# Trainium2 mixer layer: sums of weight quarters written in 64 small parts tied to the weight stream, and another order of the last seven products

## The chip, the cores and the metric

The kernel runs on one core of a Trainium2 chip. The metric is the device time of one execution in microseconds (us), as the median of several runs. A difference of 0.3% (about 4 us) is about what a measurement of this kernel can tell from no change.

## The reference, cut to what matters

One layer with a token length S of 512 and a width D of 2048. What matters here is the end of it:

```
mod = silu(c) @ w_ada + b_ada;  shift, scale, gate = split(mod, 3)
h = rmsnorm(x, norm_pre) * (1 + scale) + shift
proj = h @ w_in                      # q, f, v, z_a, v_b, z_b, g_a, g_b
...                                  # recurrent mixer -> y_a, pooling mixer -> y_b
merged = sigmoid(g_a) * (y_a @ w_proj_a) + sigmoid(g_b) * (y_b @ w_proj_b)
out = merged @ w_out                 # 512x2048 times 2048x2048
x = x + gate * rmsnorm(out, norm_post)
```

## The kernel before, in words

Each float32 product is made as three products of rounded halves: a block of weights of 512 KB is loaded by SyncE (SP) into a tile `raw`, ScalarE (ACT) rounds it into `hi` (L177), VectorE (DVE) subtracts to get `lo` (L178), and TensorE (PE) multiplies hi by hi, hi by lo and lo by hi (L91). `w_piece` does this; each of `raw`, `hi` and `lo` has four buffers, and the blocks of all stages go through them in one line. Every engine and every DMA queue works through its own list in order.

The stage of the gates (tiles `g_ps`, stored as `sig`) is the columns g_a and g_b of `h @ w_in`: sixteen steps, (b, m) with b of 0 and 1 and m of 0, 2, to 14, each of four blocks (96 matmuls). The first of them and four steps for z_a (`za`) come earlier; fifteen follow without another stage between them. Into these steps two more streams are laid. The rows of the adaLN gate: 64 loads of 256 KB into tiles `gw`, six behind the four weight blocks of a step on SP's queue (`gate_rows`), each of which DVE multiplies into the tile `gate` (L621, L623); in DVE's list they stand between the `lo` of the weight blocks. After each sixteen rows `gate_finish` sends two small matmuls (`gate_ps`), eight in all. And the sums of quarters of w_out, which the last stage needs: for each half pr of the output columns four DRAM tiles `wsum` of 1024x512, named f12, f3, f4, f2, made by a plain DMA from DRAM to DRAM and then one that adds onto it, both on GpSimd's (POOL) queue (L882). f3 adds f12, and f4 adds f3. Two such DMAs are issued in each of eight steps, 2 MB each, 16 in all; nothing ties them to the progress of PE.

Then y_a and y_b (tiles `y`, 16 loads of 256 KB on POOL's queue, L892) are split, and the stage `pa`/`pb` multiplies them by w_proj_a and w_proj_b, with the same weight stream of 512 KB blocks and no `gw`.

The last stage is `merged @ w_out` by Strassen-Winograd: for each half of the columns seven products, numbered 1 to 7, of four weight blocks and 48 matmuls each, in the order of the table `ORDER`. Products 1, 2, 3 and 6 read parts of `merged` or w_out as they are; 4, 5, 6 and 7 need token operands `op4`, `op3`, `op1`, `op2`, which `op_34`, `op_2`, `op_1` compute on DVE and ACT during the first half. A finished product is added into the output tiles `og` (rows of tokens t, 0 to 3, and column blocks j) as `INTO` says. As soon as an `og` tile is complete its squares are summed on ACT (L1069) and it is multiplied by the gate on DVE (L1070). As soon as the four tiles of a t are complete, `finish` takes the root of the mean square (ACT L248, DVE L249 to L252), multiplies and adds x again (L1031, four instructions), and stores (L1032). x comes by `x_again` on POOL's queue. The last product of all, number 4 of the second half, loads all its four blocks first and does all of its first token tile (t 0) before the second (t 1).

Of the kernel before, what the change touches and what calls it, by code (L numbers as in the profile page):

```python
# [9 lines left out]
F32 = mybir.dt.float32  # L10
# [3 lines left out]
ALU = mybir.AluOpType  # L14

P = 128
D = 2048
S = 512
KT = D // P
# [6 lines left out]
ZA_AT = 2  # L26
# [8 lines left out]
def trunk(ctx, tc, x, c, w_ada, b_ada, norm_pre, norm_post, w_in, lower_bounds, hgrn_norm,  # L35
          pool_w, pool_scale, w_proj_a, w_proj_b, w_out, out):
    nc = tc.nc
# [3 lines left out]
    const = ctx.enter_context(tc.tile_pool(name="const", bufs=1))  # L41
# [8 lines left out]
    def t_h(name, dt=F32R):  # L50
        return act.tile([P, S], dt, tag="h", bufs=32, name=name)

    def t_s(name, dt=F32):
        return act.tile([P, S], dt, tag="s", bufs=32, name=name)

    def t_w(name, n=S, dt=F32):
        return act.tile([P, 544], dt, tag="w", bufs=10, name=name)[:, :n]
# [8 lines left out]
        return pg.tile([P, S], F32, tag="pg", name=name)  # L66

    last_load, last_pool = [None], [None]

    def load(dst, src):  # L70

        if last_load[0] is None:
            d = nc.sync.dma_start(dst, src)
        else:
            with tc.issue_after(last_load[0]):
                d = nc.sync.dma_start(dst, src)  # L76
        last_load[0] = ins_of(d)
# [4 lines left out]
    def ins_of(d):  # L82
        return getattr(d, "ins", d)
# [38 lines left out]
    def finish_heads(n):  # L122
        while steps and len(heads_done) < n:
            tick(1)
# [12 lines left out]
    scan_mask = const.tile([P, S], F32, name="scan_mask")  # L137
# [33 lines left out]
    def w_piece(name, src, k0, nk, c0, n, eng=None):  # L171

        raw = ring.tile([P, nk, n], F32, tag="raw", bufs=4, name=f"{name}_raw")
        load(raw, src[k0 * P:(k0 + nk) * P, c0:c0 + n].rearrange("(k p) n -> p k n", p=P))
        hi = ring.tile([P, nk, n], F32R, tag="whi", bufs=4, name=f"{name}_hi")
        lo = ring.tile([P, nk, n], F32R, tag="wlo", bufs=4, name=f"{name}_lo")
        last_w[0] = ins_of(nc.scalar.copy(hi, raw))  # L177
        (eng or (nc.gpsimd if steps and next(turn) else nc.vector)).tensor_sub(lo, raw, hi.bitcast(F32))  # L178
        return hi, lo

    def split(name, src, alloc, eng=None):
# [81 lines left out]
    with tc.high_priority():  # L263
        for t in range(TT):
            for j in range(4):
                junk = t_w(f"junk_{t}_{j}")
# [69 lines left out]
    def in2(name, c0):  # L336
        outs = [t_ps(f"{name}_ps0"), t_ps(f"{name}_ps1")]
        proj2(name, w_in, KT, c0, hh, hl, outs)
        return outs
# [227 lines left out]
    def gate_a(h, p):  # L567
        sz = t_w(f"sza_{h}")
        nc.scalar.activation(sz, p, AF.Silu)
        sz_a[h] = sz  # L570

    def finish_a(h):
        y = o_sb[h]
        nc.vector.scalar_tensor_tensor(y, y, vec[:, R_HN + h:R_HN + h + 1], sz_a[h], op0=ALU.mult, op1=ALU.mult)
        last_pool[0] = ins_of(nc.gpsimd.dma_start(y_dram[0][h], y))
# [38 lines left out]
    def gate_rows(j, k):  # L614

        if k == 0:
            gate[j] = t_w(f"gate_{j}")
        t = t_w(f"gw_{j}_{k}")
        load(t, w_ada[k * P:(k + 1) * P, 2 * D + j * S:2 * D + (j + 1) * S])
        if k == 0:  # L620
            nc.vector.tensor_scalar(gate[j], t, c_act[:, 0:1], None, op0=ALU.mult)  # L621
        else:
            nc.vector.scalar_tensor_tensor(gate[j], t, c_act[:, k:k + 1], gate[j], op0=ALU.mult, op1=ALU.add)  # L623
# [40 lines left out]
    for k0 in range(2, KT, 2):  # L664
        first, last = (needs[k0 - 2] if k0 > 2 else 1) + 1, needs[k0]
# [25 lines left out]
    start, t = [], 0.0  # L691
# [6 lines left out]
    for it in seq:  # L698
        if it[0] == "w":
            n = it[1]  # L700
# [58 lines left out]
    for n, (name, k0, k_first, k_last) in enumerate(chunks):  # L759
        t, fresh, ends = start[n], needs[k0] == n, k0 + 1 == k_last  # L760
# [84 lines left out]
    HK = D // 2  # L845
    wsum = [[dram.tile([HK, S], F32, name=f"wsum_{i}_{pr}") for i in range(4)] for pr in range(2)]
    quarter = lambda pr, i, j: w_out[i * HK:(i + 1) * HK, (2 * pr + j) * S:(2 * pr + j + 1) * S]
    wsum_steps = []
    for pr in range(2):
        f12, f3, f4, f2 = wsum[pr]  # L850
        for dst, first, second in ((f12, quarter(pr, 0, 1), quarter(pr, 1, 1)), (f3, quarter(pr, 0, 0), f12),
                                   (f4, quarter(pr, 1, 0), f3), (f2, quarter(pr, 0, 0), quarter(pr, 0, 1))):
            wsum_steps += [(dst, first, {}), (dst, second, {"accum_op": ALU.add, "max_dma_last_dim": 8192})]

    wsum_steps = [s for pr in range(2) for acc in (0, 1) for s in wsum_steps[8 * pr + acc:8 * pr + 8:2]]

    sig = [[None] * KT, [None] * KT]
    for b, off in ((0, OFF_GA), (1, OFF_GB)):
        for m in range(0, KT, 2):
            if (b, m) == (0, ZA_AT):  # L860
                for h in range(0, NH, 2):
                    o2 = in2(f"za{h}", OFF_ZA + h * P)
                    gate_a(h, o2[0]); gate_a(h + 1, o2[1])
                    if h < 6:
                        finish_heads(h + 2)
                        finish_a(h); finish_a(h + 1)
            o2 = in2(f"g{b}_{m}", off + m * P)
            if (b, m) == (0, ZA_AT + 2):
                finish_heads(NH)
                finish_a(6); finish_a(7)  # L870

            first = ZA_AT // 2 + 2
            step = b * KT // 2 + m // 2 - first
            for i in range(max(0, step * GATE_PER), min(4 * KT, (step + 1) * GATE_PER)):
                gate_rows(i // KT, i % KT)
                if i % KT == KT - 1:
                    gate_finish(i // KT)
            if b * KT + m >= 8 and wsum_steps:
                for _ in range(2):
                    dst, src, kw = wsum_steps.pop(0)  # L880
                    with tc.issue_after(last_pool[0]):
                        last_pool[0] = ins_of(nc.gpsimd.dma_start(dst, src, **kw))  # L882
            for r in range(2):
                sig[b][m + r] = t_s(f"sig{b}_{m + r}")
                nc.scalar.activation(sig[b][m + r], o2[r], AF.Sigmoid)
# [94 lines left out]
    xr = [[None] * 4 for _ in range(TT)]  # L980
    ss = [const.tile([P, 4], F32, name=f"ss_{t}") for t in range(TT)]
    ms3 = [const.tile([P, 1], F32, name=f"ms3_{t}") for t in range(TT)]
    junk = const.tile([P, S], mybir.dt.bfloat16, name="ojunk")

    def product(pr, n, banks, last):
        form, b = PRODUCTS[n]
# [47 lines left out]
    def t_acc(pr, block, name):  # L1034
        return t_s(name) if pr == 0 else t_h(name, F32) if block == (0, 0) else t_w(name)

    def x_again(t):
        for j in range(4):
            xr[t][j] = t_h(f"xr_{t}_{j}", F32)
            nc.gpsimd.dma_start(xr[t][j], x[t * P:(t + 1) * P, j * S:(j + 1) * S])  # L1040

    ORDER = [[1, 3, 2, 4, 5, 7, 6], [1, 3, 6, 2, 7, 5, 4]]
    after = {(0, 1): op_34, (0, 3): op_2, (0, 2): op_1, (1, 6): lambda: x_again(2), (1, 2): lambda: None,
             (1, 7): lambda: (x_again(3),), (1, 5): lambda: (x_again(0), x_again(1))}
    for pr, order in enumerate(ORDER):
        left = {blk: sum(b == blk for n in order for b, _ in INTO[n]) for blk in ((0, 0), (0, 1), (1, 0), (1, 1))}
        banks, begun = {}, set()
        for n in order:
            alloc = t_pg if n in (1, 3) else t_ps
            banks[n] = banks[ONTO[n]] if n in ONTO else [alloc(f"out_{pr}_{n}_{tt}") for tt in range(2)]  # L1050
            for tt in product(pr, n, banks, (pr, n) == (1, 4)):
                p = banks[n][tt]
                for (i, jj), sign in INTO[n]:
                    t, j = 2 * i + tt, 2 * pr + jj
                    if ((i, jj), tt) not in begun:
                        begun.add(((i, jj), tt))
                        og[t][j] = t_acc(pr, (i, jj), f"og_{t}_{j}")
                        if sign > 0:
                            nc.scalar.copy(og[t][j], p)
                        else:  # L1060
                            nc.scalar.activation(og[t][j], p, AF.Copy, scale=-1.0)
                    elif sign > 0:
                        nc.vector.tensor_add(og[t][j], p, og[t][j])
                    else:
                        nc.vector.tensor_sub(og[t][j], og[t][j], p)
                    left[i, jj] -= 1 if tt else 0
                    if left[i, jj] == (0 if tt else 1):
                        at_ss = place(t, j)
                        nc.scalar.activation(junk, og[t][j], AF.Square, accum_out=ss[t][:, at_ss:at_ss + 1])  # L1069
                        nc.vector.tensor_mul(og[t][j], og[t][j], gate[j])  # L1070
                        if pr == 1 and at_ss == 2:
                            first_sums(t)
                        if at_ss == 3:
                            finish(t)
            after.get((pr, n), lambda: None)()


# [27 lines left out]
```

## Time and profile before

| | |
|---|---|
| time, median of 3 runs | 1421.37 us (1418.52 to 1421.98) |
| time of the profiled execution | 1424.94 us |
| its span, first to last instruction | 1423.2 us |
| busy: PE, DVE, ACT, POOL | 93%, 57%, 39%, 17% |
| mean granted TensorE clock | 0.974 |
| moved by DMA | 238.11 MB, mean 167 GB/s |

Busy shares are over the whole span. The stages have different limits, so a share says little of one stage. A clock of 1.00 is the higher of TensorE's two levels, 2.4 GHz, and 0.50 the lower, 1.2 GHz; a number between them is a mean over a stretch. The DMA share is the mean over 16 engines, and can pass 1.00 since the packets of one engine overlap a little.

### The profile page before, as it was taken

How to read it: one execution, taken by the hardware profiler on the slowest of the kernel's cores; microseconds unless marked ns; L12 is line 12 of the kernel's file. 1: busy time of each engine (PE TensorE's matmuls, PEld its weight loads, DVE VectorE, ACT ScalarE, POOL GpSimd, SP SyncE). 2: the span in 40 equal slices, each digit the busy share in tenths (PEclk: the TensorE clock that was granted, in tenths of full speed). 3: DMA queues.
4: the chain of work that ended last, by engine and by line, in shares of the span. 5: the costliest groups of instructions: out<-in, count | busy, mean ns of one | idle time of the engine just before them, and what ended most of it. 6: DMA issues, size and time to landing. Idle time of an engine off the chain costs nothing.

```text
span 1423.2 us, 16399 instructions
## 1 busy us (share of the span) xinstructions
PE 1328.0 (93%) x6031; PEld 1091.8 (77%) x6031; DVE 812.6 (57%) x1336; ACT 559.2 (39%) x787; POOL 246.3 (17%) x269
## 2 busy tenths in 40 slices
PE   4899999999999999999997737999999999999996
PEld 2777888888888887888876525888888888887885
DVE  4789462474957869668422223454335554587667
ACT  5544452364554564546411111222234222255552
POOL 3555401132232222223101000000001000000010
PEclk9999999999999999999998868999999999999998
DMA  9989533222223233242399999865435333336675
GB/s 310 357 271 358 183 90 104 84 74 75 86 85 111 73 97 104 75 133 89 119 327 255 286 277 248 239 192 162 156 122 166 97 96 97 104 127 199 196 255 214
DMA packets 170232, 238.11 MB, mean 167 GB/s; under 512 B 8780, under 2 KB 120484, under 8 KB 169128
## 3 DMA queue, kind: packets, MB, share of 16 engines
q1 hardware_dynamic: 155528, 188.78, 41.7%
q0 software_dynamic: 13312, 46.14, 12.0%
q10 hardware_dynamic: 1312, 2.14, 0.4%
q8 instruction: 47, 0.77, 0.2%
q14 instruction: 33, 0.27, 0.1%
HBM read 228.64 MB, written 41.94 MB: 190 GB/s over the span
## 4 chain that ended last, share of the span: by engine, by line
PE 76%; DMA 14%; DVE 7%; issue 1%; SPq 1%; ACT 1%; POOL 0%; DVEq 0%; ACTq 0%
PE g_ps L91 18%; PE out L91 8%; DMA gw<-in_w_ada_dram 8%; PE vb_ps L91 6%; PE za_ps L91 6%; PE v_ps L91 6%; PE pb L91 6%; PE pa L91 6%; PE g L91 5%; PE zb_ps L91 5%; DMA ada<-in_w_ada_dram 4%; PE q_ps L91 3%; PE lv L91 2%; DMA g_raw<-in_w_in_dram 1%; SPq L76 1%
## 5 line engine op out<-in xcount | busy, mean ns | idle before, releaser
L91 PE MATMUL g_ps<-h_hi,g_lo 128*128 128x512 f32 x512 | 205.3, 401 | 53.5 <-DVE g_lo L178 53.5
L91 PE MATMUL g_ps<-h_hi,g_hi 128*128 128x512 f32 x512 | 204.5, 399 | 0.0
L91 PE MATMUL g_ps<-h_lo,g_hi 128*128 128x512 f32 x512 | 203.2, 397 | 0.0
L177 ACT CAST g_hi<-g_raw 128x1024 fp32r<-128x1024 f32 x64 | 67.0, 1050 | 238.8 <-DMA g_raw<-in_w_in_dram 112.8
L91 PEld LDWEIGHTS g_ps<-h_hi,g_lo 128*128 128x128 f32 x512 | 98.8, 193 | 77.9 <-DVE g_lo L178 57.0
L623 DVE SCALAR_TENSOR_TENSOR gate<-gw,c_act,gate 128x512 f32<-128x512 f32 x60 | 45.1, 751 | 151.7 <-DMA gw<-in_w_ada_dram 150.7
L91 PEld LDWEIGHTS g_ps<-h_lo,g_hi 128*128 128x128 f32 x512 | 98.8, 193 | 21.2
L91 PEld LDWEIGHTS g_ps<-h_hi,g_hi 128*128 128x128 f32 x512 | 99.0, 193 | 20.6
L178 DVE TENSOR_TENSOR g_lo<-g_raw,g_hi 128x1024 fp32r<-128x1024 f32 x61 | 73.7, 1220 | 64.4 <-ACT g_hi L177 64.4
L178 DVE TENSOR_TENSOR wo_lo<-wo_raw,wo_hi 128x1024 fp32r<-128x1024 f32 x56 | 68.2, 1223 | 43.8 <-ACT wo_hi L177 43.6
L177 ACT CAST wo_hi<-wo_raw 128x1024 fp32r<-128x1024 f32 x56 | 59.0, 1054 | 68.2 <-PE out L91 51.5
L105 DVE SCALAR_TENSOR_TENSOR ada_acc<-ada,c_act,ada_acc 128x512 f32<-128x512 f32 x104 | 73.3, 750 | 7.8 <-DMA ada<-in_w_ada_dram 7.3
L1040 POOL DMA_DIRECT2D xr<-in_x_dram x16 | 8.7, 548 | 306.2 <-PE out L91 305.8
L91 PE MATMUL vb_ps<-h_hi,vb_hi 128*128 128x512 f32 x128 | 51.5, 402 | 0.0
L91 PE MATMUL out<-wo_lo,op_hi 128*128 128x512 f32 x128 | 49.9, 390 | 1.3 <-DVE wo_lo L178 1.3
L91 PE MATMUL za_ps<-h_hi,za_hi 128*128 128x512 f32 x128 | 51.1, 399 | 0.0
L91 PE MATMUL zb_ps<-h_hi,zb_hi 128*128 128x512 f32 x128 | 50.9, 398 | 0.0
L91 PE MATMUL v_ps<-v_hi,h_hi 128*128 128x512 f32 x128 | 50.5, 394 | 0.0
L91 PE MATMUL vb_ps<-h_hi,vb_lo 128*128 128x512 f32 x128 | 50.1, 391 | 0.0
L91 PE MATMUL za_ps<-h_hi,za_lo 128*128 128x512 f32 x128 | 50.0, 391 | 0.0
L91 PE MATMUL vb_ps<-h_lo,vb_hi 128*128 128x512 f32 x128 | 50.0, 390 | 0.0
L91 PE MATMUL zb_ps<-h_hi,zb_lo 128*128 128x512 f32 x128 | 49.9, 390 | 0.0
(343 smaller groups left out, 3269.9 us busy)
## 6 DMA issues: line engine op xcount, KB each, us to landing
ada<-in_w_ada_dram SPq DMA_DIRECT2D x128, 256.0 KB, 6.6
g_raw<-in_w_in_dram SPq DMA_DIRECT2D x64, 512.0 KB, 4.6
wsum<-in_w_out_dram POOLq DMA_DIRECT2D x12, 2048.0 KB, 36.0
gw<-in_w_ada_dram SPq DMA_DIRECT2D x64, 256.0 KB, 6.5
wo_raw<-wsum SPq DMA_DIRECT2D x32, 512.0 KB, 4.0
wo_raw<-in_w_out_dram SPq DMA_DIRECT2D x24, 512.0 KB, 4.6
v_raw<-in_w_in_dram SPq DMA_DIRECT2D x16, 512.0 KB, 3.6
vb_raw<-in_w_in_dram SPq DMA_DIRECT2D x16, 512.0 KB, 3.7
```

Source lines behind the costliest of these rows:

```text
L76: d = nc.sync.dma_start(dst, src)
L91: d = nc.tensor.matmul(o, lhsT, rhs, start=start, stop=stop, skip_group_check=onto)
L105: d = f(*args, **kw)
L177: last_w[0] = ins_of(nc.scalar.copy(hi, raw))
L178: (eng or (nc.gpsimd if steps and next(turn) else nc.vector)).tensor_sub(lo, raw, hi.bitcast(F32))
L623: nc.vector.scalar_tensor_tensor(gate[j], t, c_act[:, k:k + 1], gate[j], op0=ALU.mult, op1=ALU.add)
L1040: nc.gpsimd.dma_start(xr[t][j], x[t * P:(t + 1) * P, j * S:(j + 1) * S])
```

## The change

The 16 DMAs of 2 MB become 64 of 512 KB (256 rows of 512 columns), with rows cut at 1 KB for plain and adding ones alike. They are in a list that is filled once, after step (0, 4). From then on every `w_piece` takes one: POOL first copies one column of the block's `hi` into a small tile `token`, and so waits for ACT's rounding of that block, and then issues the part. For each half pr, the 16 plain parts (f12, f3, f4, f2, four each) come first, then the 16 that add. The first part goes with the first block of step (0, 6), the last with a block of the third pair of `pb`.

In the last stage the second half does its products in the order 1, 3, 6, 7, 5, 2, 4 instead of 1, 3, 6, 2, 7, 5, 4, so that the tiles of t 2 and t 3 are complete one product earlier. In the first half `op_2` comes after product 2 instead of 3, and `op_1` after 4 instead of 2. The loads of x come at other products, and the squares go to a tile that has no other use by then.

```diff
+    wsum_steps, token = [], const.tile([P, 1], F32, name="token")
+    def paced(hi):
+        if wsum_steps:
+            dst, src, kw = wsum_steps.pop(0)
+            with tc.issue_after(last_pool[0]):
+                t = ins_of(nc.gpsimd.tensor_copy(token, hi[:, 0, 0:1].bitcast(F32)))
+            with tc.issue_after(t):
+                last_pool[0] = ins_of(nc.gpsimd.dma_start(dst, src, max_dma_last_dim=1024, **kw))
...
         (eng or (nc.gpsimd if steps and next(turn) else nc.vector)).tensor_sub(lo, raw, hi.bitcast(F32))
+        paced(hi)
...
-        for dst, first, second in ((f12, quarter(pr, 0, 1), quarter(pr, 1, 1)), (f3, quarter(pr, 0, 0), f12),
-                                   (f4, quarter(pr, 1, 0), f3), (f2, quarter(pr, 0, 0), quarter(pr, 0, 1))):
-            wsum_steps += [(dst, first, {}), (dst, second, {"accum_op": ALU.add, "max_dma_last_dim": 8192})]
-    wsum_steps = [s for pr in range(2) for acc in (0, 1) for s in wsum_steps[8 * pr + acc:8 * pr + 8:2]]
+        sums = ((f12, quarter(pr, 0, 1), quarter(pr, 1, 1)), (f3, quarter(pr, 0, 0), f12),
+                (f4, quarter(pr, 1, 0), f3), (f2, quarter(pr, 0, 0), quarter(pr, 0, 1)))
+        for i, kw in ((1, {}), (2, {"accum_op": ALU.add})):
+            for s in sums:
+                wsum_later += [(s[0][r:r + 2 * P], s[i][r:r + 2 * P], kw) for r in range(0, HK, 2 * P)]
...
-            if b * KT + m >= 8 and wsum_steps:
-                for _ in range(2):
-                    dst, src, kw = wsum_steps.pop(0)
-                    with tc.issue_after(last_pool[0]):
-                        last_pool[0] = ins_of(nc.gpsimd.dma_start(dst, src, **kw))
+            if (b, m) == (0, ZA_AT + 2):
+                wsum_steps += wsum_later
...
-    junk = const.tile([P, S], mybir.dt.bfloat16, name="ojunk")
+    junk = scan_mask
...
-    ORDER = [[1, 3, 2, 4, 5, 7, 6], [1, 3, 6, 2, 7, 5, 4]]
-    after = {(0, 1): op_34, (0, 3): op_2, (0, 2): op_1, (1, 6): lambda: x_again(2), (1, 2): lambda: None,
-             (1, 7): lambda: (x_again(3),), (1, 5): lambda: (x_again(0), x_again(1))}
+    ORDER = [[1, 3, 2, 4, 5, 7, 6], [1, 3, 6, 7, 5, 2, 4]]
+    after = {(0, 1): (op_34,), (0, 2): (op_2,), (0, 4): (op_1,), (1, 6): (lambda: x_again(2),),
+             (1, 7): (lambda: x_again(3), lambda: x_again(0)), (1, 5): (lambda: x_again(1),)}
```

On POOL, in the stage of the gates, the DMAs of the first half stood in one block with nothing between them (before; `wsum_0` is the first half, and what follows it is one of the four tiles):

```order
L882 DMA wsum_0_4756<-wsum_0_4755 256x2048
L882 DMA wsum_0_4757<-wsum_0_4756 256x2048
L882 DMA wsum_0_4758<-in_w_out_dram 1024x512
L882 DMA wsum_1_4759<-in_w_out_dram 1024x512
L882 DMA wsum_1_4760<-in_w_out_dram 1024x512
```

Now each part has a copy of one block's `hi` ahead of it (the names g_14 and g_0 are steps (0, 14) and (1, 0), the number after them the block):

```order
L76 COPY token<-g_14_8_hi 128x1
L78 DMA wsum_0_4756<-in_w_out_dram 256x2x256
L76 COPY token<-g_14_12_hi 128x1
L78 DMA wsum_0_4756<-in_w_out_dram 256x2x256
L76 COPY token<-g_0_0_hi 128x1
L78 DMA wsum_0_4757<-wsum_0_4756 512x256
L76 COPY token<-g_0_4_hi 128x1
L78 DMA wsum_0_4757<-wsum_0_4756 512x256
```

So one step of the gates carries four parts, and the adding ones have rows of 256 elements, 1 KB.

On DVE, at the change to the last product, number 4, the `lo` of its blocks stood ahead of what `finish` does for t 2 and t 3 (before; `out_1_0` is the bank of product 5's sum, and some rows of 128x1 and the later of eight `og` rows are not shown):

```order
L178 TENSOR_TENSOR wo_4_0_lo<-wo_4_0_raw,wo_4_0_hi 128x1024
L178 TENSOR_TENSOR wo_4_2_lo<-wo_4_2_raw,wo_4_2_hi 128x1024
L178 TENSOR_TENSOR wo_4_4_lo<-wo_4_4_raw,wo_4_4_hi 128x1024
L1065 TENSOR_TENSOR og_3_10108<-og_3_10108,out_1_0_9870 128x512
L1065 TENSOR_TENSOR og_3_10112<-og_3_10112,out_1_1_9871 128x512
L178 TENSOR_TENSOR wo_4_6_lo<-wo_4_6_raw,wo_4_6_hi 128x1024
L1070 TENSOR_TENSOR og_3_10108<-og_3_10108,gate_7399 128x512
```

Now three of the four stand behind it, and behind the sums of product 2 (`out_2`), which is the product before (the last of the eight `og` rows of `finish` and what follows):

```order
L1040 SCALAR_TENSOR_TENSOR og_3_10224<-og_3_10224,ro_10428,xr_3_10320 128x512
L1074 TENSOR_TENSOR og_2_10308<-og_2_10308,out_2_0_10452 128x512
L1072 TENSOR_TENSOR og_3_10218<-out_2_0_10452,og_3_10218 128x512
L1074 TENSOR_TENSOR og_2_10311<-og_2_10311,out_2_1_10453 128x512
L1072 TENSOR_TENSOR og_3_10222<-out_2_1_10453,og_3_10222 128x512
L1079 TENSOR_TENSOR og_3_10218<-og_3_10218,gate_7458 128x512
L1031 TENSOR_REDUCE ms_0_9352<-ss_9348 128x1
L188 TENSOR_TENSOR wo_4_2_lo<-wo_4_2_raw,wo_4_2_hi 128x1024
L1032 TENSOR_SCALAR ms_0_9352<-ms_0_9352 128x1
L1079 TENSOR_TENSOR og_3_10222<-og_3_10222,gate_7458 128x512
L1031 TENSOR_REDUCE ms_1_9353<-ss_9349 128x1
L188 TENSOR_TENSOR wo_4_4_lo<-wo_4_4_raw,wo_4_4_hi 128x1024
```

`wo_4_0_lo` is earlier, between product 5's sums and the eight `og` rows. On ACT the rounding of block `wo_4_0` now stands between the squares of t 2 and t 3 and the load of the root's table:

```order
L1078 ACTIVATE scan_mask,ss_9351<-og_3_10224 128x512
L187 CAST wo_4_0_hi<-wo_4_0_raw 128x1024
L259 ACT_TABLE_LOAD
L259 ACTIVATE ro_r<-ro_v_10405 128x1
L259 ACTIVATE ro_r<-ro_v_10426 128x1
```

The lists of DVE and ACT in the stage of the gates, and SP's list there, are as before.

## Rows read from the trace of the kernel before

**Rows 1.** Waits of PE: who waited for whom, us in total, times, longest.

```profile
PE g_ps L91 <- DVE g_lo L178: 53.5, 8, 22.3
PE out L91 <- DVE wo_lo L178: 1.3, 1, 1.3
```

**Rows 2.** Stretches: length, busy us of PE, PEld, DVE, ACT, POOL, clock, DMA share, GB/s.

```profile
708.50:887.80 179.30, 125.83 (x510) 100.55 (x508) 45.45 (x53) 27.92 (x33) 13.39 (x14) 0.86 1.02 279
887.80:909.50 21.70, 21.70 (x83) 17.68 (x84) 9.07 (x11) 5.49 (x7) 0.00 (x0) 0.86 0.92 252
953.00:974.80 21.80, 21.80 (x98) 17.99 (x97) 9.36 (x11) 5.31 (x6) 0.00 (x0) 1.00 0.53 168
1060.00:1082.00 22.00, 22.00 (x99) 18.21 (x98) 14.27 (x18) 14.10 (x21) 5.48 (x10) 1.00 0.65 210
1104.00:1148.00 44.00, 44.00 (x196) 36.44 (x195) 22.36 (x30) 11.40 (x13) 0.00 (x0) 1.00 0.32 96
```

**Rows 3.** Groups of instructions on PE from 684 to 1082.4.

```profile
L91 PE MATMUL g_ps<-h_hi,g_lo 128*128 128x512 f32 x480 | 192.8, 402 | 53.5 <-DVE g_lo L178 53.5
```

**Rows 4.** Chain of work that ended last: start, us, what; from 680 to 1110.

```profile
684.06 3.44 PE g_ps L91 x15
...
691.39 1.77 PE o L91 x14
...
1082.38 10.88 PE pa L91 x48
```

**Rows 5.** The same chain from 735 to 800.

```profile
774.59 21.50 DMA gw<-in_w_ada_dram
...
796.86 1.23 DVE g_lo L178
```

**Rows 6.** DMA issues from 708.5 to 887.8: times, KB each, median us to landing.

```profile
gw<-in_w_ada_dram SPq DMA_DIRECT2D x30, 256.0 KB, 20.9
```

**Rows 7.** DMA issues from 953 to 997.

```profile
gw<-in_w_ada_dram SPq DMA_DIRECT2D x12, 256.0 KB, 5.4
```

**Rows 8.** DMA queues from 745 to 752: packets, MB, share of 16 engines.

```profile
q0 software_dynamic: 529, 1.08, 83.1%
q1 hardware_dynamic: 530, 0.53, 27.9%
```

**Rows 9.** DMA queues from 757.6 to 773.6.

```profile
q0 software_dynamic: 272, 2.10, 63.4%
```

**Rows 10.** DMA queues from 710 to 719.

```profile
q0 software_dynamic: 613, 2.44, 88.9%
```

**Rows 11.** PE in order of time, two matmuls behind a gap (in brackets) and the last.

```profile
738.80 0.50 PE L91 MATMUL g_ps<-h_hi,g_lo 128*128 128x512 f32 x1 [2.45 <-DVE g_lo L178]
...
761.94 0.79 PE L91 MATMUL g_ps<-h_hi,g_lo 128*128 128x512 f32 x1 [6.53 <-DVE g_lo L178]
...
1409.96 0.39 PE L91 MATMUL out<-wo_hi,op_lo 128*128 128x512 f32 x1
```

**Rows 12.** DVE in order of time from 1399.

```profile
1399.02 1.28 DVE L1065 TENSOR_TENSOR og<-og,out 128x512 f32<-128x512 f32 x2
...
1404.34 5.39 DVE L1031 SCALAR_TENSOR_TENSOR og<-og,ro,xr 128x512 f32<-128x512 f32 x8
1409.64 1.44 DVE L1063 TENSOR_TENSOR og<-out,og 128x512 f32<-128x512 f32 x2
1411.18 0.69 DVE L1070 TENSOR_TENSOR og<-og,gate 128x512 f32<-128x512 f32 x1
...
1413.38 2.73 DVE L1031 SCALAR_TENSOR_TENSOR og<-og,ro,xr 128x512 f32<-128x512 f32 x4
...
1416.41 2.74 DVE L1031 SCALAR_TENSOR_TENSOR og<-og,ro,xr 128x512 f32<-128x512 f32 x4
```

**Rows 13.** ACT in order of time from 1399.

```profile
1399.51 1.06 ACT L177 CAST wo_hi<-wo_raw 128x1024 fp32r<-128x1024 f32 x1 [1.67 <-PE out L91]
...
1401.96 1.28 ACT L248 ACT_TABLE_LOAD   x1
```

More of the change, by code (lines that the diff above doesn't have):

```diff
@@ L847, in trunk @@
     quarter = lambda pr, i, j: w_out[i * HK:(i + 1) * HK, (2 * pr + j) * S:(2 * pr + j + 1) * S]
-    wsum_steps = []
+    wsum_later = []
     for pr in range(2):
         f12, f3, f4, f2 = wsum[pr]
-        for dst, first, second in ((f12, quarter(pr, 0, 1), quarter(pr, 1, 1)), (f3, quarter(pr, 0, 0), f12),
-                                   (f4, quarter(pr, 1, 0), f3), (f2, quarter(pr, 0, 0), quarter(pr, 0, 1))):
-            wsum_steps += [(dst, first, {}), (dst, second, {"accum_op": ALU.add, "max_dma_last_dim": 8192})]
-    wsum_steps = [s for pr in range(2) for acc in (0, 1) for s in wsum_steps[8 * pr + acc:8 * pr + 8:2]]
+        sums = ((f12, quarter(pr, 0, 1), quarter(pr, 1, 1)), (f3, quarter(pr, 0, 0), f12),
[3 more added lines that the diff above has]
+                wsum_later += [(s[0][r:r + 2 * P], s[i][r:r + 2 * P], kw) for r in range(0, HK, 2 * P)]
     sig = [[None] * KT, [None] * KT]
@@ L1074, in trunk @@
                             finish(t)
-            after.get((pr, n), lambda: None)()
+            for f in after.get((pr, n), ()):
+                f()
 _INS = ["x", "c", "w_ada", "b_ada", "norm_pre", "norm_post", "w_in", "lower_bounds", "hgrn_norm",
```

## The prediction

> **What bounds the kernel now.** I read the waits of PE first, since PE is busy 93% of the span and everything else is meant to hide behind it. The reader is to see that one wait is large: in eight places PE waited, 53.5 us in total, for the `lo` of a gate block; the only wait in the last stage is 1.3 us [rows 1]. Next the stretches, to see when. From 708.5 to 887.8 PE is busy 125.83 of 179.30 us, the clock is 0.86 in the mean and the DMA engines are full, 1.02; in the step from 953 the same work with the same `gw` loads, but no sums, runs without a gap at clock 1.00 and a DMA share of 0.53 [rows 2]. So the stall belongs to the stretch in which the sums move.
>
> How much the stage loses in all, clock included, follows from counting. It has three groups of 480 matmuls (one stands in [rows 3]) and ends where `pa` begins. A matmul at full clock takes 10.88 us / 48 = 0.227 us [rows 4], so 1440 take 326.4 us, the eight `gate_ps` 1.8 us and the last head's matmuls 1.8 us [rows 4]. From 684.06 to 1082.38 are 398.3 us [rows 4]. **398.3 - 326.4 - 1.8 - 1.8 = 68.3 us are lost**, 53.5 us of it as gaps, the rest at the lower clock behind them.
>
> Then the chain, for the way it happens: a load of `gw` takes 21.50 us, then comes one `lo`, then PE [rows 5]. In DVE's list the multiplications of `gw` stand between the `lo` of weight blocks, and on SP's list the six `gw` of a step stand behind the weights that the last `lo` sets free. So each step of the gates has a loop, `lo` to SP to `gw` to DVE to the next `lo`, which must fit into the 21.76 us that PE needs for 96 matmuls. With the sums beside it a `gw` lands 20.9 us after its issue [rows 6], without them 5.4 us [rows 7]. The first breaks the loop, the second fits.
>
> Why they are so late is in the queues: from 745 to 752 the engines took 529 packets of POOL's queue (q0) and 530 of SP's (q1) [rows 8]. They take turns packet by packet, and q0's were larger. With packets of 8 KB it is worse: 2.10 MB in 272 [rows 9].
>
> **What the change does to this stage.** It moves the same bytes in 64 parts, one for each block of 24 matmuls, 5.44 us. What a part costs the engines depends on its packets.
>
> Plain: 613 packets of together 2.44 MB took 88.9% of 9 us on 16 engines, that is 209 ns for 4 KB [rows 10]. A part of 512 KB is 128 of these, 1.7 us of all engines; as packets of 1 KB at the price of the weights' (below, 55 ns) 1.8 us. Either way small.
>
> Adding: 2 KB packets took 0.831 x 7 x 16 / 529 = 176 ns [rows 8], 8 KB packets 0.634 x 16 x 16 / 256 = 634 ns (256 of the 272 carry 2.10 MB) [rows 9]. No row shows 1 KB. The straight line through the two is 24 ns + 76 ns for each KB, so 100 ns; the lower bound is half a 2 KB packet, 88 ns, the upper one a whole, 176 ns. I take 100 ns, an estimate, since the two sizes are nearly in proportion. A part is then 512 x 100 / 16 = 3.2 us.
>
> The rest of the load: weights and `gw` together take 0.53 x 21.8 = 11.5 us of a step, weights alone 0.32 [rows 2]. Two queues together can show more than one: 83.1% + 27.9% = 1.11 [rows 8]; I divide by 1.1.
>
> - Steps with plain parts: (11.5 + 4 x 1.7) / 1.1 = 16.6 us of 21.76. No wait.
> - The four steps (0, 14) to (1, 4) with adding parts and `gw`: (11.5 + 4 x 3.2) / 1.1 = 22.1 us, 0.35 us too much each: **+1.4 us**.
> - Step (1, 14) with adding parts and the loads of `y`: (0.65 x 22 [rows 2] + 12.8) / 1.1 = 24.6, 2.6 us over 22. `lo` is made three blocks (16 us) ahead of PE, which can swallow this, so 0 to 2.6: **+1.3 us**.
> - `pa`/`pb` with twelve adding parts: 0.32 x 21.76 + 12.8 = 19.8, /1.1 = 18.0. No wait.
>
> The `gw` loop in the fullest step: when both queues are full, turns are about 160 / 1.1 = 145 ns long and SP's queue gets one packet in each, where 8 KB packets gave it one in some 700 ns. A block ahead and the first `gw` are 32 + 8 packets per engine, 5.8 us; the next five `gw` another 5.8 us; with the start of the transfer (under 5.4 us, [rows 7]) and three `lo` of 1.23 us [rows 5] it is about 20 us, just inside 21.76.
>
> The Trainium skill (DMA: Bandwidth & Descriptors, section SWDGE vs HWDGE vs iDMA) says that GpSimd's descriptors are gathered into packets of preferably up to 4096 B, and that an engine changes queues only between packets. Our plain rows of 2 KB did become 4 KB packets [rows 10], the adding ones did not (1.08 MB in 529, [rows 8]). By that rule adding parts would come in packets of 24 + 4 x 76 = 328 ns, 2.6 us a part, and the +1.4 us would be 0.
>
> POOL's new copies: 64 of 128x1, with nothing behind them but more parts and the loads of `y`. They read `hi`, so a buffer of `hi` is free only after POOL has passed; ACT writes it four blocks later, 22 us. That covers the copy; if POOL stands still longer, ACT, `lo` and PE stand too (a rival below). SP's list is not touched.
>
> **Last stage, first half.** `op_2` and `op_1` come a product later, so the `lo` of product 4 no longer waits behind them: **-1.3 us** [rows 1]. Their users, products 7 and 6, are one or more products of 10.88 us behind.
>
> **Last stage, the end.** Let E be the end of product 2, now the last but one; product 5 ends at E - 10.88. Before, product 5 ended about 1409.96 + 0.39 - 10.88 = 1399.5 [rows 11], and the eight `og` rows of t 2 and t 3 were done at 1404.34 + 5.39 = 1409.7 [rows 12], 10.2 us later. Now ACT first rounds `wo_4_0`, 1.06 us [rows 13], which waits for PE to pass the first block of product 2 (2.7 us), and only then loads the root's table, which began at 2.5 us before [rows 13]: 1.3 us later, so DVE is free at E + 0.7. Then come four sums (1.28 + 1.44), one gate row (0.69) [rows 12] and `wo_4_2_lo` (1.23): E + 5.4. PE wants it after seven matmuls, at E + 1.6: a wait of 3.8 us. `wo_4_4_lo` is ready one gate row and one `lo` later, E + 7.4; PE wants it at E + 6.8: 0.6 us. The fourth is in time. **+4.4 us**, a wait that was not there. It is given back in part: before, DVE reached the sums of t 0 only at 1409.64, behind the eight `og` rows, and the last `og` row ended at 1419.15, 8.8 us after PE [rows 11, 12]. Now t 0, ready 5.44 us before PE's end, has DVE for itself: some 3.0 us from its sum to its first `og` row (1409.64 to 1413.38 less the 0.7 us of t 1's sum) and 2.7 us for four, so it ends 0.3 us after PE; t 1 needs the same 5.7 us, so the last row ends 6.0 us after PE: **-2.8 us**. Net **+1.6 us**; bounds -2.8 (no wait) and, if the clock falls behind the wait, about +5: 3.8 us lies between gaps of 2.45 and 6.53 us [rows 11] in a stretch whose clock is 0.86 in the mean, and the rows do not say which of them brought it down. A fall costs some 3 us (0.14 of 21.7 at 0.86, [rows 2]).
>
> The squares' other target tile is the same instruction: nothing.
>
> **Sum.** -68.3 + 1.4 + 1.3 - 1.3 + 1.6 = -65.3 us. Against the profiled execution, 1424.94 us (span 1423.2 and 1.7 around it), that is 1359.6 us. The median of the runs shown is 3.6 us below the profiled one, so a median may be as low as 1356; I say 1359 us.
>
> **Rivals.**
> 1. *Small adding packets cost more than the line says.* At 140 ns a turn is (140 + 59) / 1.1 = 181 ns, with 59 ns for SP's packet [rows 8]; a part needs 32 turns, 5.8 us, more than a block's 5.44 us, and SP's queue gets 59 / 199 x 1.1 = 0.33 of the engines where it wants 0.53. The 16 parts beside `gw` then take 93 us at 0.62 of PE's pace, 35 us lost less the 16 us of lead, and (1, 14) some 11 us: about 1388 us. For: a packet that reads, adds and writes may have a floor. Against: 8 KB costs 3.6 times 2 KB, so there is little fixed in it.
> 2. *The same to its end, slower than before.* At the 176 ns of a 2 KB packet a part takes 32 x 235 / 1.1 = 6.8 us, SP's queue gets 0.28: 51 us lost beside `gw`, 15 in (1, 14), 10 in `pa`/`pb`, less 16: 60 us, 1420 us. From about 180 ns on the kernel is slower than before.
> 3. *POOL stands still.* The loads of `y` now stand between the copies and wait for `gate_ps` and for `y_lo`. If they hold POOL over 22 us, `hi` buffers stay taken and PE waits. They wait for PE's own progress, so I expect a few us at most: 1362 to 1380.
> 4. *The change does not do what it says*, since `gw` alone breaks the loop. Against it is the step from 953, with `gw` and no gap [rows 2]. Time 1421.
>
> **How the numbers follow.** The sum's case, with 88 to 120 ns for a packet and the bounds of the end: 0.78, range 1351 to 1370. Rival 1: 0.10. Rival 2: 0.06, half of it slower. Rival 3: 0.03. Rival 4: 0.03. A range of 1350 to 1390 leaves out rivals 2 and 4, what of rival 1 is worse than its number, and a little at the low end. Differences under 0.3% (4 us) cannot be told from none: faster 0.93, same 0.03, slower 0.04.
>
> **What would show it.** The wait of PE for `g_lo` falls from 53.5 us to under 5; the clock is 1.00 from 708 to 905; `gw` lands in 5 to 13 us all through; the stretch with adding parts has a DMA share near 1.0, the plain one near 0.85; POOL's queue shows 1 KB packets at 90 to 120 ns where it adds; in product 4 PE waits 3 to 5 us for `wo_lo`; the wait of 1.3 us in the first half is gone; the last `og` row ends 6 us after PE. The prediction is wrong if adding packets cost over 130 ns, if POOL's waits show behind `y`, or if the wait in product 4 brings the lower clock.

## The result, and the profile after

The changed kernel takes 1360.38 us (median of 4 runs, 1358.44 to 1361.33) against 1421.67 us (1418.52 to 1426.18) for the kernel before, a ratio of 0.9565 with a 95% interval of 0.9537 to 0.9593. Its profiled execution took 1361.33 us, with a span of 1359.4 us and a mean clock of 0.992. The prediction was 1359 us.

The waits of PE first (who waited for whom, us in total, times, longest), those of the stages that the change touches:

```profile
PE out L101 <- DVE wo_lo L188: 3.4, 1, 3.4
```

The 53.5 us for `g_lo` and the 1.3 us of the first half [rows 1] are gone; 3.4 us in product 4 are new. The chain of work that ended last (start, us, what) has the length of the stages:

```profile
685.55 3.44 PE g_ps L101 x15
...
699.26 97.97 PE g_ps L101 x432
...
797.71 65.33 PE g_ps L101 x288
...
1016.83 10.88 PE pa L101 x48
...
1190.91 133.29 PE out L101 x588
...
1337.31 5.77 PE out L101 x17
```

From 685.55 to 1016.83 are 331.3 us, where it was 398.3 us [rows 4]: **-67.0 us**. In the rows at 699.26 and 797.71 PE does 432 and 288 matmuls without a break; before, all eight gaps lay among these 720. `pa` and `pb` take the same 174.1 us as before. From 1190.91 to the end of the span are 168.5 us, where it was 166.7, which is 1423.2 less 1245.58 + 10.88, the end of the last `pb` in the chain before:

```profile
1245.58 10.88 PE pb L91 x48
```

So the last stage is **+1.8 us**. All that lies ahead of the gates, where nothing was changed, took 1.5 us longer in this execution. The sum is -63.7 us, the spans differ by 63.8.

The stretches of the gates (columns as in [rows 2]), one with plain and two with adding parts, and two around the new wait:

```profile
708.50:795.00 86.50, 86.50 (x383) 71.67 (x382) 36.88 (x42) 21.59 (x25) 24.12 (x30) 1.00 0.80 255
795.00:882.00 87.00, 87.00 (x385) 72.01 (x384) 34.52 (x40) 20.21 (x24) 25.62 (x30) 1.00 1.07 258
882.00:904.00 22.00, 22.00 (x99) 18.24 (x98) 8.03 (x10) 6.66 (x8) 7.54 (x10) 1.00 0.97 239
1333.93:1337.31 3.38, 0.00 (x1) 0.00 (x0) 3.38 (x8) 1.45 (x4) 0.00 (x0) 1.00 0.30 110
1337.31:1343.10 5.79, 5.79 (x18) 4.62 (x19) 3.00 (x6) 0.00 (x0) 0.00 (x0) 0.71 0.00 0
```

PE is full and the clock is 1.00 where they were 125.83 of 179.30 us and 0.86. The bytes for each microsecond are only some 10% fewer (239 to 258 GB/s against 279). What has changed is what SP's queue gets of them. The queues and DMA issues from 800 to 885, in the stretch of adding parts:

```profile
q0 software_dynamic: 7447, 7.79, 58.4%
q1 hardware_dynamic: 10970, 13.99, 49.4%
...
gw<-in_w_ada_dram SPq DMA_DIRECT2D x24, 256.0 KB, 7.4
wsum<-wsum POOLq DMA_DIRECT2D x8, 512.0 KB, 10.5
```

SP's queue has 49.4% of the engines, where it had 27.9% [rows 8], and a `gw` lands in 7.4 us instead of 20.9 [rows 6]. The end, DVE in order of time:

```profile
1327.68 5.39 DVE L1040 SCALAR_TENSOR_TENSOR og<-og,ro,xr 128x512 f32<-128x512 f32 x8
...
1336.04 1.22 DVE L188 TENSOR_TENSOR wo_lo<-wo_raw,wo_hi 128x1024 fp32r<-128x1024 f32 x1
...
1337.90 1.22 DVE L188 TENSOR_TENSOR wo_lo<-wo_raw,wo_hi 128x1024 fp32r<-128x1024 f32 x1
...
1352.57 2.74 DVE L1040 SCALAR_TENSOR_TENSOR og<-og,ro,xr 128x512 f32<-128x512 f32 x4
```

PE's last matmul:

```profile
1348.12 0.39 PE L101 MATMUL out<-wo_hi,op_lo 128*128 128x512 f32 x1
```

So the last `og` row ends 6.8 us after PE, where it was 8.8 [rows 11, 12].

### The profile page after: what moved, and what is told of

Its sections match the earlier page's. It is cut to its first block, busy times and chain, and to the rows that moved or that the text cites. A ratio compares the mean times of both kernels' runs of the same rounds, so it can differ in the third digit from the quotient of the medians.

```text
span 1359.4 us, 16610 instructions
## 1 busy us (share of the span) xinstructions
PE 1317.6 (97%) x6031; PEld 1087.5 (80%) x6031; DVE 812.0 (60%) x1336; ACT 558.9 (41%) x787; POOL 343.6 (25%) x381
## 4 chain that ended last, share of the span: by engine, by line
PE 85%; DVE 3%; ACT 0%; issue 0%; POOL 0%; DVEq 0%; ACTq 0%
PE g_ps L101 26%; PE out L101 10%; PE vb_ps L101 6%; PE za_ps L101 6%; PE v_ps L101 6%; PE pb L101 6%; PE pa L101 6%; PE zb_ps L101 5%; PE q_ps L101 3%; PE g L101 3%; PE lv L101 2%; PE o L101 1%; PE mix L101 1%; DVE og L1040 1%; DVE vb L600 1%; PE po L101 0%
## 5 line engine op out<-in xcount | busy, mean ns | idle before, releaser
L101 PE MATMUL g_ps<-h_hi,g_hi 128*128 128x512 f32 x512 | 200.3, 391 | 0.0
L101 PE MATMUL g_ps<-h_hi,g_lo 128*128 128x512 f32 x512 | 199.6, 390 | 0.0
L101 PE MATMUL g_ps<-h_lo,g_hi 128*128 128x512 f32 x512 | 199.5, 390 | 0.0
L101 PEld LDWEIGHTS g_ps<-h_hi,g_hi 128*128 128x128 f32 x512 | 96.2, 188 | 19.9
L188 DVE TENSOR_TENSOR wo_lo<-wo_raw,wo_hi 128x1024 fp32r<-128x1024 f32 x56 | 68.4, 1225 | 40.4 <-ACT wo_hi L187 40.3
L76 POOL COPY token<-g_hi 128x1 f32<-128x1 f32 x52 | 36.8, 709 | 183.6 <-ACT g_hi L187 183.5
L78 POOL DMA_DIRECT2D wsum<-in_w_out_dram x48 | 52.9, 1105 | 4.4 <-issue 4.3
L101 PE MATMUL out<-wo_hi,op_hi 128*128 128x512 f32 x128 | 50.6, 395 | 0.0
L101 PE MATMUL out<-wo_hi,op_lo 128*128 128x512 f32 x128 | 50.5, 394 | 0.0
```

The lines of the kernel that those rows point to most:

```text
L76: t = ins_of(nc.gpsimd.tensor_copy(token, hi[:, 0, 0:1].bitcast(F32)))
L78: last_pool[0] = ins_of(nc.gpsimd.dma_start(dst, src, max_dma_last_dim=1024, **kw))
L101: d = nc.tensor.matmul(o, lhsT, rhs, start=start, stop=stop, skip_group_check=onto)
```

## The experiments

The theory: what the gates lost was lost because the sums came faster than the engines could carry beside the weights and `gw`; tied to the weights they come at about half that rate. POOL's queue of the kernel before, from 708.5 to 887.8, moved 182 GB/s:

```profile
q0 software_dynamic: 8943, 32.58, 72.0%
```

Tied, a step of 21.76 us has 2.1 MB of sums, 96 GB/s. Rivals: the length of the packets is what counts, or the size of a part, or the new order. Each kernel was timed beside the kernel before (1422 to 1424 us).

| kernel | median, us | ratio to before, 95% | PE waits for `g_lo`, us | `wo_lo` |
|---|---|---|---|---|
| tied_alone | 1362.17 | 0.9516 to 0.9605 | none | 3.4 |
| tied_whole_sums | 1359.77 | 0.9529 to 0.9577 | none | 3.4 |
| tied_big_rows | 1364.89 | 0.9569 to 0.9611 | 6.3 | 3.4 |
| tied_alone_later | 1374.67 | 0.9622 to 0.9661 | 12.9 | 3.4 |
| two_parts_a_block | 1400.64 | 0.9821 to 0.9874 | 29.0 | 3.4 |
| untied_small_rows | 1410.01 | 0.9882 to 0.9927 | 40.4 | 3.4 |
| rows_of_512 | 1359.78 | 0.9507 to 0.9581 | none | 3.4 |
| no_sums | 1359.44 | 0.9531 to 0.9565 | none | 4.1 |
| order_alone | 1424.16 | 0.9999 to 1.0028 | 49.0 | 3.4 |
| sums_alone | 1357.05 | 0.9517 to 0.9550 | none | none |
| blocks_ahead | 1355.32 | 0.9509 to 0.9542 | none | 0.3 |

**Short packets without the tie.** The kernel before with rows of 1 KB (the 8192 of the adding DMAs is taken out too), and with the change's last stage.

```diff
-                        last_pool[0] = ins_of(nc.gpsimd.dma_start(dst, src, **kw))
+                        last_pool[0] = ins_of(nc.gpsimd.dma_start(dst, src, max_dma_last_dim=1024, **kw))
```

> The 16 whole DMAs of the kernel before, tied to nothing, with rows cut at 1 KB as in the change, and the change's last stage. Theory (tying counts most, the length of the packets some): POOL's queue is never empty for some 200 us. Turns of (101 + 59) / 1.1 = 145 ns leave SP's queue 0.41 of the engines in adding stretches where it wants 0.53, the plain ones 0.24 as before. The same count for the kernel before gives 93 us where 68 were measured; here it gives 68, so 50 are expected: 1390 to 1410 us. Rival 1 (small packets alone cure it): 1365 us or less. Rival 2 (packets do not matter at all): 1418 us or more.

1410.01 us, only 13 us faster, at the upper end of the theory's range and apart from both rivals. Its stretch of 708.5 to 888 (columns as above) has the engines as full as in [rows 2], and PE busy 19 us more:

```profile
708.50:888.00 179.50, 145.00 (x599) 117.05 (x598) 57.20 (x65) 31.97 (x38) 29.93 (x13) 0.90 1.08 279
```

**The tie without the small parts and the short rows.** The change, last stage included, but in `paced` only every fourth block takes a DMA, and the list holds the 16 whole ones with the rows of before.

```diff
-        if wsum_steps:
+        if wsum_steps and next(blocks) == 0:
...
-                wsum_later += [(s[0][r:r + 2 * P], s[i][r:r + 2 * P], kw) for r in range(0, HK, 2 * P)]
+                wsum_later += [(s[0], s[i], kw)]
```

> 16 whole DMAs with the rows of the kernel before (plain 2 KB, adding 2 KB from w_out and 8 KB from wsum), tied to the weights, one with every fourth block: of the change's three edits to the sums (parts, rows, tie) the tie alone, with the change's last stage. Theory (tying brings nearly all, long rows cost some microseconds): the mean load of an adding step stays under capacity, (11.5 + 4 x 2.7) / 1.1 = 20.3 of 21.76 us, but the 8 KB packets of a whole come in one stretch of 16 x 693 / 1.1 = 10.1 us, which a gw can meet whole; gw lands after over 15 us in two of the steps, 2 to 8 us lost in each: 1363 to 1376 us. Rival (without the short rows or the small parts the tie is worth little): 1385 us or more.

1362.17 us, -61 us: the tie alone brings all of the change's gain that a measurement can tell. The range was a little too high, since PE does not wait at all. The stage of the gates has the length it has with the change, 331.28 us (1018.00 - 686.72):

```profile
686.72 3.44 PE g_ps L101 x15
...
1018.00 10.88 PE pa L101 x48
```

**The tie with whole sums in short rows.** The same edit of `paced` and of the list, rows of 1 KB kept.

> 16 whole DMAs of 2 MB with rows of 1 KB, tied to the weights: one with every fourth block. Theory (the mean rate counts, not the size of a part): a step has the same bytes; a plain whole is through in 32 turns of 244 ns, 7.8 us, an adding one in 128 turns of 145 ns, 18.6 us, both inside 21.76 us, so the queue is empty again before the next: 1360 to 1366 us, gw landing under 14 us. Rival (the small parts are what spares gw): the six gw of a step stand in one full stretch, land after over 15 us, and each of the four adding steps with gw loses 3 us or more: 1372 to 1385 us.

1359.77 us, no wait: as the change. The size of a part makes no difference that can be measured here.

**Twice the rate.** A second `paced(hi)` in each block.

> Two parts with each block of weights, so the sums are done in 8 steps instead of 16. Theory (capacity of the 16 engines sets it): an adding step needs (11.5 + 8 x 3.3) / 1.1 = 34.5 us of 21.76, 12.7 too much in each of four, a plain one (11.5 + 8 x 1.7) / 1.1 = 22.8, 1 to 2 too much in each of four; 55 to 59 us less what the lead of the lo swallows (up to 16 us): 1397 to 1415 us, DMA share 1.0 and the clock under 1.00 in the adding steps. Rival (being tied to the weights is enough at any rate, since a late block holds the parts back too): 1370 us or less.

1400.64 us. Three stretches of it (columns as above): the first with plain parts, the second with the last plain and the first adding ones, the third with mostly adding ones:

```profile
717.00:752.00 35.00, 35.00 (x156) 28.97 (x155) 12.16 (x15) 8.90 (x10) 14.88 (x24) 1.00 0.95 315
752.00:795.00 43.00, 43.00 (x191) 35.62 (x190) 14.86 (x18) 10.45 (x14) 20.35 (x25) 1.00 1.10 268
795.00:838.00 43.00, 38.49 (x153) 30.48 (x152) 16.42 (x19) 7.52 (x9) 18.26 (x26) 0.92 1.17 258
```

The tie is still there, the short rows and small parts too; with the rate doubled 40 of the 61 us are lost again. So the rate is the cause, and the tie is a way to set it. What counts is the time of the DMA engines and not the bytes: plain parts at twice the rate, 315 GB/s at a share of 0.95, cost PE nothing. The tie could also do harm of its own, if a late copy on POOL kept a buffer of `hi` from ACT; but ACT waited 5.1 us in all for these copies, and in the chain from 795 to 925 loads of `gw` have 63.3%.

**Long rows in tied parts.**

```diff
-                last_pool[0] = ins_of(nc.gpsimd.dma_start(dst, src, max_dma_last_dim=1024, **kw))
+                last_pool[0] = ins_of(nc.gpsimd.dma_start(dst, src, max_dma_last_dim=8192 if kw else 1024, **kw))
```

> 64 tied parts as in the change, but the adding ones in rows as long as before (8 KB from wsum, 2 KB from w_out). Theory (tying is what counts): an 8 KB part is 64 packets of 634 ns, 4 for each engine; with one packet of SP's queue (59 ns) between them it is through in 4 x 693 / 1.1 = 2.5 us of a block's 5.44 us, and SP's queue has the rest for itself. No step is over capacity, (11.5 + 4 x 2.7) / 1.1 = 20.3 of 21.76 us: 1358 to 1362 us, no wait of PE for g_lo over 2 us. Rival (the length of a packet counts, since SP's queue gets one packet in some 700 ns beside 8 KB packets): gw lands after more than 15 us in the steps that add, at least 10 us are lost: 1370 us or more.

1364.89 us, between the two: the theory's upper end was missed by 3 us, with two waits for `g_lo` where none over 2 us was expected. POOL in order of time shows the parts in a bunch, because ACT rounded three blocks shortly after one another, from 835.68 to 839.23 (in brackets the idle time before, and what ended it):

```profile
836.86 1.17 POOL L76 COPY token<-g_hi 128x1 f32<-128x1 f32 x1 [12.56 <-ACT g_hi L187]
837.97 0.77 POOL L78 DMA_DIRECT2D wsum<-wsum  x1
...
839.15 0.77 POOL L78 DMA_DIRECT2D wsum<-wsum  x1
...
839.94 0.90 POOL L78 DMA_DIRECT2D wsum<-wsum  x1
```

Nothing for 12.56 us, then three within 2 us. With the whole DMAs of tied_alone there were no such waits, though their rows are as long. Was it the place in the step? In tied_alone POOL in order of time shows the two adding DMAs that read wsum, the second just behind a step's `gw`, and the next DMA 22 us later:

```profile
827.57 0.90 POOL L78 DMA_DIRECT2D wsum<-wsum  x1 [0.30 <-issue]
849.32 0.87 POOL L78 DMA_DIRECT2D wsum<-wsum  x1 [0.29 <-issue]
...
871.55 1.27 POOL L78 DMA_DIRECT2D wsum<-in_w_out_dram  x1 [0.29 <-issue]
```

SP's queue of tied_alone, in order of time, shows those `gw`, the weights behind them and the next `gw`:

```profile
846.96 8.62 SPq L86 DMA_DIRECT2D gw<-in_w_ada_dram  x6
855.66 15.31 SPq L86 DMA_DIRECT2D g_raw<-in_w_in_dram  x4
871.01 3.90 SPq L86 DMA_DIRECT2D gw<-in_w_ada_dram  x6
```

**The same DMAs at another place in the step**: `next(blocks) == 2` instead of 0.

> As tied_alone (16 whole DMAs, rows as before), but tied to the third block of a step instead of the first. Tied to the first, an adding DMA was issued at 849.3 us, just behind the step's gw (issued from 847.0 on), and its 10 us were over before the gw of the next step (from 871.0). Theory (where in the step the long packets fall decides whether they meet gw; that is why 64 parts with long rows lost 6.3 us, three of them issued from 838.0 to 839.9 ahead of a gw): issued some 11 us later the 8 KB packets meet the next gw, which lands after 10 us or more in two of the adding steps, 2 to 8 us lost in each: 1364 to 1378 us. Rival (the place in the step is nothing; parts are worse for their own sake): no wait of PE for g_lo, 1360.5 to 1363.5 us.

1374.67 us, 12.5 us more than tied_alone. POOL in order of time has the two adding DMAs that read wsum 12.9 and 10.2 us later than there, one ahead of a step's `gw` and the other ahead of the weights behind them:

```profile
840.49 0.91 POOL L78 DMA_DIRECT2D wsum<-wsum  x1 [0.19 <-issue]
...
859.50 0.88 POOL L78 DMA_DIRECT2D wsum<-wsum  x1 [0.29 <-issue]
```

SP's queue of this kernel, in order of time:

```profile
845.74 17.23 SPq L86 DMA_DIRECT2D gw<-in_w_ada_dram  x6
863.06 16.11 SPq L86 DMA_DIRECT2D g_raw<-in_w_in_dram  x4
```

Six `gw` that took 8.62 us to be issued now take 17.23, and with the weights behind them it is 33.3 us where it was 23.9; a step of PE has 21.76. The chain that ended last has two of these `gw`:

```profile
847.63 13.00 DMA gw<-in_w_ada_dram
...
862.64 11.29 DMA gw<-in_w_ada_dram
```

Behind the second PE waits 8.2 us, until 875.96. So with long rows the place in the step decides. Two `gw` of 10 us or more are what was expected; the median landing time of all `gw` there is 8.9 us, so it is a few that are late. A slow `gw` alone is not the loss: in the change six `gw` took 15.67 us to be issued (from 843.87), the weights behind them 10.29, and PE did not wait. That the bunch in tied_big_rows costs in the same way is likely, but was not tried by itself. Short rows at the later place were not tried either.

**The price of a packet**: rows of the adding parts cut at 512 bytes.

> The change with the rows of the adding parts cut at 512 bytes. It tests the price of a packet, on which the prediction's sum rested. Theory (the straight line through 2 KB and 8 KB, 24 ns + 76 ns for each KB, goes on): 62 ns a packet, 4.0 us a part; an adding step with gw needs (11.5 + 4 x 4.0) / 1.1 = 25.0 us, 3.2 too much, but turns are as short as SP's own packets and the plain parts behind have room, so POOL's queue lags more than SP's: 1360 to 1372 us. Rival (a packet that adds has a floor near that of 1 KB, 95 to 105 ns): a part takes 6.5 us, a step (11.5 + 26) / 1.1 = 34 us, 12 too much in each of four and 9 or more in (1, 14) and pa/pb, less 16 us of lead: 1390 us or more.

No wait, 1359.78 us, just under the theory's range. The queues from 800 to 885:

```profile
q0 software_dynamic: 14592, 7.63, 71.0%
q1 hardware_dynamic: 11115, 14.14, 49.2%
```

0.710 x 85 x 16 / 14592 = 66 ns for 0.5 KB, where the line through 2 KB and 8 KB gave 62. The rival's floor is not there. SP's queue keeps its 49%.

**What the sums still cost.** Products 2, 4, 5 and 7, all that read a sum, read a quarter of w_out instead, and the list stays empty.

> The change without the sums: products 2, 4 and 7 read one quarter of w_out as it is, so all 64 parts, their copies on POOL and what they move are left out, and the output is not the layer's. It measures what the sums still cost. Theory: 1.3 us, all in the stage of the gates (331.3 us against 330.0): 1357 to 1360.5 us, stage of the gates 329.5 to 330.5 us. Rival (the parts still cost much that the gaps of PE do not show, by the clock or by late weights): 1355 us or less.

The stage of the gates is 1017.54 - 686.26 = 331.28 us, to 0.01 us as with the change, not the 329.5 to 330.5 that were expected:

```profile
686.26 3.44 PE g_ps L101 x15
...
1017.54 10.88 PE pa L101 x48
```

So the sums cost this stage nothing now; it was my count of the stage without loss that was 1.3 us short (below).

**The order of the last products.** First the change's last stage on the kernel before:

> The kernel before with the change's last stage alone (orders of the products, op_1 and op_2 later, loads of x, target of the squares); the sums as before. Theory: the stage of the gates stays as it was; the last stage loses the 1.3 us wait and gains a wait of PE for wo_lo of 3.4 us with 1.9 us of lower clock behind it, less 2.0 us at the tail: 168.5 us instead of 166.7 between pa/pb and the end, time 1422 to 1425 us. Rival (the new order pays, as the shorter tail outweighs the wait): the last stage is 165 us or less, time 1417 to 1420 us.

1424.16 us; the ratio, 0.9999 to 1.0028, can't be told from no change. The profile shows 167.4 us from the end of `pb` to the end (1421.0 less 1253.61), 0.7 more than before, and PE in order of time in product 4:

```profile
1400.03 0.50 PE L91 MATMUL out<-wo_lo,op_hi 128*128 128x512 f32 x1 [3.39 <-DVE wo_lo L178]
1400.36 0.39 PE L91 MATMUL out<-wo_hi,op_lo 128*128 128x512 f32 x1
...
1401.89 0.50 PE L91 MATMUL out<-wo_lo,op_hi 128*128 128x512 f32 x1 [0.20 <-DVE ms L1023]
```

The wait is there, the lower clock behind it is not. Then the change with the old order of the second half, and the loads of x where they were:

```diff
-    ORDER = [[1, 3, 2, 4, 5, 7, 6], [1, 3, 6, 7, 5, 2, 4]]
+    ORDER = [[1, 3, 2, 4, 5, 7, 6], [1, 3, 6, 2, 7, 5, 4]]
```

> The change with the second half's products and the loads of x in the order before (1, 3, 6, 2, 7, 5, 4); the sums and op_1, op_2 as changed. Theory: no wait of PE in product 4 and no lower clock, -3.4 and -1.9 us, and the longer tail, +2.0 us: 1357 us (1355.5 to 1359). Rival (the new order of the last products pays): 1361 us or more. The last og row ends 8.8 us after PE by the first.

1357.05 us, as the theory said, no wait, and the last `og` row ends at 1347.62 + 2.74, 8.8 us after PE's last matmul (1341.17 + 0.39):

```profile
1189.24 141.45 PE out L101 x624
```

All 624 matmuls in one piece (141.45 / 624 = 0.2267 us each). The intervals of this kernel and of the change do not quite exclude each other (0.9517 to 0.9550 and 0.9537 to 0.9593), but the profile gives the 3 us their place: the last stage is 165.3 us (1354.5 less 1189.24), where the change has 168.5.

**The new order without its wait.** The change's order, with product 4's blocks written ahead of product 2's sums:

```diff
+            if (pr, n) == (1, 2):
+                ahead.extend(w_piece(f"wo_1_4_{k}", wsum[1][2], k, 2, 0, S) for k in range(0, KH, 2))
             yield 0
...
-            ws = [piece(k) for k in range(0, KH, 2)]
+            ws = ahead or [piece(k) for k in range(0, KH, 2)]
```

> The change with the four blocks of product 4 written ahead of the sums of product 2, so that wo_4_2_lo, wo_4_4_lo and wo_4_6_lo come on DVE behind the eight og rows and ahead of those sums. With E the end of product 2, DVE is free at E + 0.7, wo_4_2_lo ready at E + 1.9 (wanted at E + 1.6), wo_4_6_lo at E + 4.4 (wanted at E + 4.4). Theory: PE waits 0.3 to 0.6 us instead of 3.4 and keeps its clock; DVE reaches the sum of t 0 at E + 7.9 instead of E + 10.75, and all behind it is 3 us earlier: 1357 us, last og row some 9 us after PE. Rival (DVE is the chain at the end anyway, its work only changes places): within 1 us of the change, 1359.5 to 1361 us.

1355.32 us where 1357 was expected, the lowest median of all, 5 us under the change; from sums_alone (0.9517 to 0.9550) it can't be told. DVE now makes the three `lo` at once behind the eight `og` rows:

```profile
1332.74 3.49 DVE L188 TENSOR_TENSOR wo_lo<-wo_raw,wo_hi 128x1024 fp32r<-128x1024 f32 x3
...
1348.72 2.74 DVE L1044 SCALAR_TENSOR_TENSOR og<-og,ro,xr 128x512 f32<-128x512 f32 x4
```

PE's last matmul:

```profile
1343.21 0.39 PE L101 MATMUL out<-wo_hi,op_lo 128*128 128x512 f32 x1
```

PE waits 0.3 us and ends 4.9 us earlier than with the change, and the last `og` row ends 7.9 us after it instead of 6.8, where some 9 were expected.

## Why the prediction was right, step by step

**The stage of the gates.** The step that carries the forecast, that the loss of 68.3 us is the sums' and goes away, holds: -67.0 measured. It is 1.3 us less because the count of the stage without loss was too low: `state` x4 (0.45) and `ms` x2 (0.48) stand in it too and were left out, the 1440 matmuls took 326.7 instead of 326.4, the `gate_ps` 1.9 instead of 1.8. That is 331.3 instead of 330.0, the length that the stage has without sums. `gw` landed in 3.8 to 14.9 us from 708 to 905, a little wider than the 5 to 13 that were named.

**What the sums cost beside it.** +1.4 and +1.3 were forecast, 0 was measured (no_sums). The price of a packet was right: 0.584 x 85 x 16 / 7447 = 107 ns for 1 KB against 100. What was mis-sized is the capacity: I divided by 1.1 from one row, and two_parts_a_block showed a share of 1.17 with the same packets, rows_of_512 1.20 with shorter ones (71.0% + 49.2%). With 1.17 the fullest step needs (11.5 + 4 x 3.4) / 1.17 = 21.5 us of 21.76, an estimate. Also, where there is only a little too much, it is POOL's queue that lags and not SP's, which the formula cannot see: with the change a part that adds landed after 10.5 us, twice a block's 5.44, beside `gw` of 7.4 us (rows above), and in rows_of_512 after 13.9 us, beside `gw` of 7.6 us. How much of the forecast 2.7 us each of the two explains was not separated.

The Trainium skill (DMA: Bandwidth & Descriptors, section SWDGE vs HWDGE vs iDMA) has GpSimd's descriptors gathered into packets of preferably up to 4096 B. For the plain parts the trace agrees; POOL's queue from 710 to 795, 3.6 KB a packet:

```profile
q0 software_dynamic: 2083, 7.55, 29.5%
```

For parts that add, packets were not filled up to that size, as the prediction had taken the rule: 7.79 MB in 7447 packets, 1.05 KB each, and half of it when the rows are halved (7.63 MB in 14592). The rule would have made the +1.4 us a 0, and 0 was measured, but not in this way.

**Why SP's queue was starved.** The prediction told it by turns and the length of q0's packets. The turns are right as far as they go [rows 8], but the length was the smaller matter: short packets without the tie gave 13 us, the tie with the long ones gave 61. Before, POOL issued four DMAs at once and more before they were through, so its queue had work for some 180 us, 72.0% of the engines; tied, 2.1 MB come in 21.76 us. Where in a step they come decides with long rows; with short ones it was not tried.

**The last stage.** The 1.3 us wait is gone, as forecast. In product 4 PE waited 3.4 us where 3.8 + 0.6 were forecast. The tail after PE is 6.8 us, 2.0 less than before, where 2.8 less were forecast. The clock did fall: 0.71 from 1337.31 to 1343.10, and 17 matmuls took 5.77 us where at full clock they take 3.85: +1.9 us. The prediction had left this out of its sum and named it as a sign of being wrong, and by that sign this step failed: the end, forecast at +1.6, came to some 3.3 us (3.4 + 1.9 - 2.0), inside its bounds. The stage is 1.8 us longer instead of 0.3.

**The sum.** That the whole came out so close is in part luck: the gates gave 1.4 us more than forecast (-67.0 against -65.6), the last stage took 1.5 us more, and the two nearly cancel.

**The rivals.** Small packets cost 107 ns, not 140 or 176. POOL did not stand still: its sixteen loads of `y` waited 14.4 us in all, ACT waited 5.0 us for POOL's copies, in three places, and PE, in the stages that the change touches, for no `hi`. And `gw` alone does not break the loop: beside it and the slower sums PE waits for no `g_lo`.

The new order of the last products has given nothing: on the kernel before it can't be told from no change (order_alone), and the change is 3.3 us faster without it (sums_alone). The 61 us are the gain of the sums, less what the order took.

## What to carry to other kernels

A large transfer that nothing waits for soon should be given a rate, and a cheap way to do it is to let each piece wait for a step of the stream that must not be late. Choose the rate by the fullest step (its load against the share that the queues reach together), and then the place within the step, away from the loads that have the least time, above all if the packets are long. When work is moved ahead of the last stage's end, look at what stands behind it on the same engine: here the blocks of the last product, 3.4 us, given back by writing them earlier.

## What the hardware showed that was not expected

The same wait of 3.4 us in product 4, with PE full before it, was followed by the lower clock in six profiled executions and not in three others. With the change the 5.8 us behind it ran at 0.71 in the mean, in tied_big_rows at 0.72, in tied_alone_later, two_parts_a_block, untied_small_rows and rows_of_512 at 0.71; in order_alone (rows above), tied_whole_sums and tied_alone the matmuls did not slow down. The stretch behind the wait in tied_alone, columns as above:

```profile
1338.40:1344.00 5.60, 5.33 (x22) 4.11 (x23) 3.77 (x8) 0.06 (x1) 0.00 (x0) 1.00 0.00 0
```

What makes the difference stays open; some 2 us of the difference between single executions is this. And two queues together reached a share of 1.20 in rows_of_512 and 1.17 in two_parts_a_block, not the 1.11 of [rows 8].
